# Norm factor and index relu applied in PSUM, forgetting rows as products over 32 partitions, T5 rows copied in two halves

## The chip, the cores and the metric

One core of a Trainium2 chip. The metric is the device time of one execution in microseconds; the kernel before was timed three times, and a further execution of it was profiled.

## The reference

One layer of a decoder trunk over 512 tokens of width 1024, everything in float32:

```
xn = rmsnorm(x, norm_mix_g)
sb, moba, fox, dsa and index parts = split(xn @ w_in)
o_sb   stick-breaking attention        4 heads of 64
o_mb   block-sparse attention, T5 bias 4 heads
o_fx   softmax(q k / 8 + c[t] - c[s]) v, c = cumsum(log_sigmoid(f))   4 heads
o_ds   I[t,s] = sum_h w[t,h] relu(q_idx[t,h] . k_idx[s]);  top 128 keys of I per query,
       softmax with T5 bias over them  4 heads, shared k and v
x  = x + (sum_i sigmoid(xn @ w_gate[i]) * (o_i @ w_branch[i])) @ w_out
x  = x + conv_ffn(rmsnorm(x, norm_ffn_g));   out = rmsnorm(x, norm_final_g)
```

## The kernel before

Activations lie with channels on the partitions and the 512 tokens along the free dimension. Products keep float32 accuracy by halves: an operand is split into a rounded high part (a cast on ScalarE) and the rest (a difference on VectorE or GpSimd), and three products are summed. A dense tile is 8 x 3 matmuls of 128x128 against 512 columns (`dense_steps`, L116). Weights are loaded by SyncE into two raw buffers `wr` and split into three pairs `wh`, `wl` (L91 to L104).

The stages: load and norm of x with the first value projection; then index and key projections; then the attention, in which 16 heads (F0, S0, F1, S1, M0, M1, D0, D1, two heads each) are worked off in steps n = 0, 1, 2, ..., with dense tiles of the projections and gates put between their parts; then the branch, output and feed-forward products. TensorE's order is that of the program text (`manual_schedule`); on the other engines and on SyncE's queue a planner sets the order by priorities and readiness.

In a step, `slot(n, pos, us)` (L662) runs what is due of earlier heads (transposes one step later, products with the values two steps later), then `dense(us)` of projections in the order of `ORDER`; between the slots stand the four score tiles of the step's head and, while there are any, index scores: `IXN` (L882) says how many behind each of the first positions, and the last entry holds for all later ones. When the 24 index scores are given out, the steps of the top-k search (L430) start. `QUOTA` gives the dense time of each slot.

PSUM has two banks "mm" for the dense tiles, used in turn, and six "a" for everything else.

- `factored` (L263) multiplies a projection's bank by the norm factor `rstd` into an SBUF tile `t...` of the ring "ir" (three buffers). `qtile`, `ktile` and `ixtile` (L311 to L340) cast that tile into halves on ScalarE and take the differences on VectorE (L317, L319, L329, L339); for k a transfer per head then fills the other 64 partitions (L330).
- `index_score` (L413): one matmul into a bank `ip`, a relu on ScalarE into an "ir" tile, then on VectorE a product with the head's weight added to `isc` (L423, L425).
- Forgetting rows: the cumulated logarithms `ch` and their negatives `cn` stand on partitions 96 to 99. `fox_rows` (L389) transfers them to rows 0 to 3 of each of four groups of 32 partitions, in `ck` and `cr`; for each head, VectorE multiplies `cr` by a column that is one in the head's group and zero elsewhere (L395). L458 adds the product `cq[h]` x `ck` over 128 partitions to the scores.
- `ix_spread` (L403) reads the index rows back from DRAM (`iqd`) by eight transfers. The T5 rows `brd` are copied to 128 rows for each of eight heads in `bdram` (L625), from where `bias_head` (L397) reads a head's matrix; the first is read at step 6.

Of the kernel before, what the change touches and what calls it, by code (L numbers as in the profile page):

```python
# [16 lines left out]
P = 128  # L17
# [32 lines left out]
def trunk(ctx: ExitStack, tc: tile.TileContext, xt, wv0, wv, wp, wdk, wg, wb, wo, wu, wd,  # L50
# [14 lines left out]
    ident = cst[:, 0:P]  # L65
    onesd = cst[:, 3 * P:4 * P]
    gn = cst[:, 4 * P:4 * P + 3 * KT]
    rowm = cst[:, 4 * P + 3 * KT:NCST]
    trir = cp.tile([P, P], F32R, name="trir")
    idr = cp.tile([P, P], F32R, name="idr")  # L70
    mskr = cp.tile([P, P], F32R, name="mskr")
# [3 lines left out]
    dpool = ctx.enter_context(tc.tile_pool(name="dpool", bufs=1, space=bass.MemoryType.DRAM))  # L75
    iqd = dpool.tile([8, 32, 2, S], F32, name="iqd")
    brd = dpool.tile([8, 640], F32, name="brd")
    bdram = dpool.tile([8, P, 640], F32, name="bdram")
    V.memset(eps, EPS)
    V.memset(one1, 1.0)  # L80
    V.memset(fr(negr), -1.0)
# [97 lines left out]
    with ExitStack() as ph:  # L179
# [80 lines left out]
            yield from dense_steps(ps[:m], hi, lo, blocks_of(xhi), blocks_of(xlo))  # L260
            return ps[:m]

        def factored(ps, name):  # L263
            m = ps.shape[0]
            t = pp.tile([P, S], F32, name=f"t{name}", tag="ir", bufs=3)
            V.tensor_tensor(out=t[:m], in0=ps, in1=rstd[:m], op=OP.mult)
            return t

        def drain(gen):
            while True:  # L270
                try:
                    next(gen)
                except StopIteration as e:
                    return e.value
# [4 lines left out]
        T.matmul(ms, onesd, sqa, start=True, stop=True)  # L279
        dkp = drain(dk)  # L280
        rms_rstd(ms, S, "m", pp, rstd, tag="ot")
        dkp = factored(dkp, "dk")
        for tt in range(NB):
            jk = pp.tile([P, P], F32, name=f"jk{tt}", tag="ot")
            V.tensor_tensor_reduce(out=jk, in0=rstd[:, tt * P:(tt + 1) * P], in1=ident, scale=1.0, scalar=0.0,
# [23 lines left out]
        qk, kdma = {}, [None]  # L309

        def qtile(name, scale):  # L311
            ps = factored((yield from proj(name)), name)
            q = pp.tile([P, 2, S], F32R, name=f"q{name}", tag="q", bufs=2)
            qk[name] = q
            A.activation(q[0:64, 0], ps[0:64], AF.Copy, scale=scale)
            A.activation(q[64:128, 1], ps[64:128], AF.Copy, scale=scale)
            V.scalar_tensor_tensor(out=q[64:128, 0], in0=ps[0:64], scalar=scale, in1=fr(q[0:64, 0]),  # L317
                                   op0=OP.mult, op1=OP.subtract)
            V.scalar_tensor_tensor(out=q[0:64, 1], in0=ps[64:128], scalar=scale, in1=fr(q[64:128, 1]),  # L319
                                   op0=OP.mult, op1=OP.subtract)  # L320

        def ktile(name):
            ps = factored((yield from proj(name)), name)
            k = pp.tile([P, 2, 2, S], F32R, name=f"k{name}", tag="k", bufs=2)
            qk[name] = k
            for h in range(2):
                r, o = slice(64 * h, 64 * h + 64), slice(64 - 64 * h, 128 - 64 * h)
                A.copy(k[r, h, 0], ps[r])
                V.tensor_tensor(out=k[r, h, 1], in0=ps[r], in1=fr(k[r, h, 0]), op=OP.subtract)  # L329
                kdma[0] = SP.dma_start(fr(k[o, h]), fr(k[r, h]))  # L330
# [2 lines left out]
        iq = {}  # L333

        def ixtile(c):
            t = factored(drain(proj(f"ix{c}")), f"ix{c}")
            hl = pp.tile([P, 2, S], F32R, name=f"iqs{c}", tag="lo", bufs=HB)
            A.copy(hl[:, 0], t)
            V.tensor_tensor(out=hl[:, 1], in0=t, in1=fr(hl[:, 0]), op=OP.subtract)  # L339
            SP.dma_start(iqd[4 * c:4 * c + 4].rearrange("h b x s -> (h b) x s"), fr(hl))  # L340
# [37 lines left out]
        A.copy(ch[R4, 0], fw[R4, 0])  # L378
        V.tensor_tensor(out=ch[R4, 1], in0=fw[R4, 0], in1=fr(ch[R4, 0]), op=OP.subtract)
        A.activation(cn[R4], fr(ch[R4]), AF.Copy, scale=-1.0)  # L380
        cr = pp.tile([P, S], F32, name="cr", tag="mix", bufs=KT)
        ck = pp.tile([P, S], F32R, name="ck", tag="mix", bufs=KT)
        cq = [pp.tile([P, S], F32R, name=f"cq{h}", tag="mix", bufs=KT) for h in range(4)]
        G.memset(cr, 1.0)
        G.memset(fr(ck), 1.0)

        ixtile(1)

        def fox_rows():  # L389

            for r in range(2):
                SP.dma_start(cr[2 + r:P:32], fr(cn[96:100, r]))
                SP.dma_start(fr(ck[r:P:32]), fr(ch[96:100, r]))
            for h in range(4):
                V.tensor_scalar(out=cq[h], in0=cr, scalar1=rowm[:, h:h + 1], scalar2=None, op0=OP.mult)  # L395

        def bias_head(h):  # L397
            e = pp.tile([P, S], F32, name=f"e{h}", tag="e", bufs=3)
            r = bdram[h].rearrange("p y -> (p y)")
            SP.dma_start(e, r[127:127 + P * 639].rearrange("(p y) -> p y", y=639)[:, :S])  # L400
            return e

# [10 lines left out]
        def index_score(i, h):  # L413
            n = P * (i + 1)
            if h == 0:
                isc[i] = pp.tile([P, n], F32, name=f"isc{i}")
            t = isc[i]
            ps = bank(f"ip{i}{h}")[:, :n]
            T.matmul(ps, iq[h][:, i * P:(i + 1) * P], ixk[:, :n], start=True, stop=True)
            r = pp.tile([P, S], F32, name=f"ir{i}{h}", tag="ir", bufs=3)[:, :n]  # L420
            A.activation(r, ps, AF.Relu)
            if h == 0:
                V.tensor_scalar(out=t, in0=r, scalar1=ixw[:, i, 0:1], scalar2=None, op0=OP.mult)  # L423
            else:
                V.scalar_tensor_tensor(out=t, in0=r, scalar=ixw[:, i, h:h + 1], in1=t, op0=OP.mult, op1=OP.add)  # L425
            if h == 7:
                G.affine_select(out=t[:, i * P:], in_=t[:, i * P:], pattern=[[-1, P]], base=0, channel_multiplier=1,
                                compare_op=OP.is_ge, fill=INADM)
# [15 lines left out]
        def softmax_head(b, h, q, k, v, bias, fox=False):  # L444
            p, hh = divmod(h, 2)
            nm = "FMSD"[b] + str(h)

            def scores():
                z = pp.tile([P, ALLQ], F32, name=f"z{nm}", tag="z", bufs=2)
                st = pp.tile([P, 3, NB], F32, name=f"st{nm}", tag="st", bufs=2)  # L450
                for i in range(NB):
                    n = P * (i + 1)
                    qs = slice(i * P, (i + 1) * P)
                    ps = bank(f"s{nm}{i}")[:, :n]
                    T.matmul(ps, q()[:, hh, qs], k()[:, 0, :n], start=True, stop=False)
                    T.matmul(ps, q()[:, hh, qs], k()[:, 1, :n], start=False, stop=not fox)
                    if fox:
                        T.matmul(ps, cq[h][:, qs], ck[:, :n], start=False, stop=True)  # L458
                    zz = z[:, QOFF[i]:QOFF[i] + n]
                    anchor[0] = V.tensor_tensor_reduce(out=zz, in0=ps, in1=bias(hh, i, n), scale=1.0, scalar=3e38,  # L460
                                           op0=OP.add, op1=OP.min, accum_out=st[:, 0, i:i + 1])
                    last_exp[0] = A.activation(zz, zz, AF.Exp, scale=-1.0, bias=st[:, 0, i:i + 1],
                                               accum_out=st[:, 1, i:i + 1])
                    V.reciprocal(st[:, 2, i:i + 1], st[:, 1, i:i + 1])
                    G.tensor_tensor(out=zz, in0=zz, in1=st[:, 2, i:i + 1].to_broadcast([P, n]), op=OP.mult)
                    yield
                box["z"] = z

            def turn():
                z = box["z"]  # L470
                ph_ = pp.tile([P, ALLQ], F32R, name=f"ph{nm}", tag="hi", bufs=HB)
                pl_ = pp.tile([P, ALLQ], F32R, name=f"pl{nm}", tag="lo", bufs=HB)
                for j in range(NB):
                    n = S - P * j
                    pt = bank(f"pt{nm}{j}")[:, :n]
                    for i in range(j, NB):
                        T.transpose(pt[:, (i - j) * P:(i - j + 1) * P],  # L477
                                    z[:, QOFF[i] + P * j:QOFF[i] + P * (j + 1)], ident)
                    sl = slice(KOFF[j], KOFF[j] + n)
                    A.copy(ph_[:, sl], pt)  # L480
                    anchor[0] = V.tensor_tensor(out=pl_[:, sl], in0=pt, in1=fr(ph_[:, sl]), op=OP.subtract)
                box["w"] = ph_, pl_

            box = {}
            return scores, turn, lambda: pv(b, p, hh, v(), *box["w"], nm)
# [134 lines left out]

        step = [-1]
        fox_rows()
        ix_spread()
        require("F0k")
        SP.dma_start(bdram, brd.rearrange("p (o y) -> p o y", o=1).to_broadcast([8, P, 640]))  # L625
        oTf = pp.tile([P, 2, S], F32, name="oTf")
        oTr = pp.tile([P, 3, 2, S], F32, name="oTr", tag="oT3")
        oT = [oTf, oTr[:, 0], oTr[:, 1], oTr[:, 2]]
# [46 lines left out]
        n = 0  # L675
        while due or n < len(heads):
            step[0] = n
            for h in EBIAS.get(n, ()):
                with tc.issue_after(kdma[0].ins):
                    ebias[h] = bias_head(h)  # L680
# [199 lines left out]
QUOTA = [1.5, 0.5, 2, 0.5, 1, 1]  # L880

LAG = [((1, 1), (2, 1)), ((1, 3), (2, 3))]  # L882
IXN = [0, 2, 3, 3, 2]
TKS = [1.2] * 16
EBIAS = {6: (0, 1), 8: (2,), 10: (3,), 11: (4, 5), 12: (6,), 14: (7,)}
NCST = 4 * P + 3 * KT + 4

# ---- launch
# [93 lines left out]
```

## Time and profile before

| | us |
|---|---|
| median of three timed runs | 879.92 (879.18 to 881.20) |
| the profiled execution | 877.93 |
| its span | 875.9 |
| TensorE busy | 844.6 |
| VectorE busy | 559.9 |
| ScalarE busy | 398.1 |
| GpSimd busy | 164.3 |

[...] PE is TensorE's matmul part, PEld its weight loads, DVE VectorE, ACT ScalarE, POOL GpSimd, SPq SyncE's queue.

### The profile page before, as it was taken

What the parts mean: (1) busy time and instruction counts of PE and PEld (TensorE: products, weight loads), DVE (VectorE), ACT (ScalarE), POOL (GpSimd) and SP (SyncE); (2) the same over time, 40 slices, a digit from 0 to 9 for tenths busy, and PEclk for the clock granted to TensorE, in tenths of its full rate; (3) what the DMA queues carried; (4) which work ended last, traced back from release to release, by engine and by line L of the source; (5) the groups of instructions that cost most, each with busy time, mean ns of one, the idle gap of its engine ahead of it and who ended that gap; (6) DMA issues with size and microseconds to landing.
All of it is one profiled execution on the core that took longest, in us unless ns stands there. A gap on an engine that the chain in (4) does not pass through costs nothing.

```text
span 875.9 us, 10670 instructions
## 1 busy us (share of the span) xinstructions
PE 844.6 (96%) x4040; PEld 710.4 (81%) x4040; DVE 559.9 (64%) x933; ACT 398.1 (45%) x608; POOL 164.3 (19%) x119
## 2 busy tenths in 40 slices
PE   8968999999998999999999999999999999999995
PEld 7757888788887888888888888888888888888885
DVE  6845899999663458645554477777777777423334
ACT  6524776666454573223334454444444444323221
POOL 0023547357558610000001200000000000000001
PEclk9987999999999999999999999999999999999998
DMA  6577130423523234224223233233333323333222
GB/s 222 154 241 186 53 95 26 121 61 105 172 85 110 71 97 127 90 89 129 72 73 97 97 94 99 97 97 97 96 97 97 97 96 91 91 91 108 85 67 97
DMA packets 31651, 91.18 MB, mean 104 GB/s; under 512 B 3376, under 2 KB 8368, under 8 KB 31600
## 3 DMA queue, kind: packets, MB, share of 16 engines
q1 hardware_dynamic: 30512, 89.45, 33.7%
q10 hardware_dynamic: 1088, 1.05, 0.4%
q8 instruction: 32, 0.52, 0.2%
q14 instruction: 19, 0.16, 0.1%
HBM read 83.75 MB, written 5.79 MB: 102 GB/s over the span
## 4 chain that ended last, share of the span: by engine, by line
PE 76%; DVE 12%; DMA 3%; ACT 3%; issue 2%; POOL 2%; SPq 0%; DVEq 0%; ACTq 0%
PE u L122 27%; PE dg L122 18%; PE dn L823 14%; PE o L122 5%; PE b L122 5%; DVE isc L437 2%; DVE m L436 2%; PE vpsVS L303 1%; DMA cr<-cn 1%; DMA kF0k<-kF0k 1%; DVE a L522 1%; DMA xr<-in_xt 1%; POOL ep L564 1%; PE dD0q L122 1%; PE ptD L477 0%
## 5 line engine op out<-in xcount | busy, mean ns | idle before, releaser
L92 ACT CAST wh<-wr 128x1024 fp32r<-128x1024 f32 (+1 forms) x129 | 133.5, 1038 | 159.8 <-PE dn L823 70.4
L93 DVE TENSOR_TENSOR wl<-wr,wh 128x1024 fp32r<-128x1024 f32 (+2 forms) x97 | 116.4, 1201 | 140.1 <-ACT wh L92 64.5
L93 POOL TENSOR_TENSOR wl<-wr,wh 128x1024 fp32r<-128x1024 f32 x32 | 77.7, 2431 | 70.8 <-ACT wh L92 26.1
L122 PE MATMUL u<-xhi,wh 128*128 128x512 f32 x352 | 87.5, 390 | 0.0
L122 PE MATMUL u<-xlo,wh 128*128 128x512 f32 x352 | 87.1, 389 | 0.0
L122 PE MATMUL u<-xhi,wl 128*128 128x512 f32 x352 | 87.1, 389 | 0.0
L799 DVE SCALAR_TENSOR_TENSOR cv<-h,cvp,cv 128x511 f32<-128x511 f32 x88 | 66.0, 751 | 26.1 <-ACT cv L797 24.6
L122 PEld LDWEIGHTS u<-xhi,wh 128*128 128x128 f32 x352 | 66.1, 188 | 14.1 <-issue 0.5
L122 PEld LDWEIGHTS u<-xlo,wh 128*128 128x128 f32 x352 | 66.1, 188 | 13.7
L122 PEld LDWEIGHTS u<-xhi,wl 128*128 128x128 f32 x352 | 66.1, 188 | 13.7
L823 PE MATMUL dn<-mh,wh 128*128 128x512 f32 (+1 forms) x198 | 72.9, 368 | 0.0
L823 PE MATMUL dn<-ml,wh 128*128 128x512 f32 (+1 forms) x198 | 72.3, 365 | 0.0
L823 PE MATMUL dn<-mh,wl 128*128 128x512 f32 (+1 forms) x198 | 72.3, 365 | 0.0
L797 ACT ACTIVATE cv<-h,cvp 128x512 f32<-128x512 f32 x44 | 35.9, 815 | 79.9 <-DVE h L795 79.9
L835 POOL TENSOR_TENSOR x<-x,yl 128x512 f32<-128x512 f32 x2 | 3.5, 1754 | 359.8 <-issue 354.4
L122 PE MATMUL dg<-xlo,wh 128*128 128x512 f32 x256 | 66.1, 392 | 0.0
L122 PE MATMUL dg<-xhi,wh 128*128 128x512 f32 x256 | 64.9, 390 | 0.0
L122 PE MATMUL dg<-xhi,wl 128*128 128x512 f32 x256 | 64.3, 390 | 0.0
L122 PEld LDWEIGHTS dg<-xhi,wl 128*128 128x128 f32 x256 | 47.7, 188 | 9.7
L122 PEld LDWEIGHTS dg<-xhi,wh 128*128 128x128 f32 x256 | 47.8, 188 | 9.4
L122 PEld LDWEIGHTS dg<-xlo,wh 128*128 128x128 f32 x256 | 47.4, 188 | 9.5
L771 POOL TENSOR_TENSOR rstd<-rstd,sqo 128x512 f32<-128x512 f32 x7 | 9.1, 1299 | 186.8 <-ACT sqo L770 186.8
(426 smaller groups left out, 1529.2 us busy)
## 6 DMA issues: line engine op xcount, KB each, us to landing
wr<-in_wu SPq DMA_DIRECT2D x44, 512.0 KB
wr<-in_wg SPq DMA_DIRECT2D x32, 512.0 KB
wr<-in_wp SPq DMA_DIRECT2D x16, 512.0 KB
wr<-in_wd SPq DMA_DIRECT2D x16, 512.0 KB
wbr<-in_wb SPq DMA_DIRECT2D x8, 512.0 KB
wr<-in_wo SPq DMA_DIRECT2D x8, 512.0 KB
wr<-in_wd SPq DMA_DIRECT2D x8, 384.0 KB
bdram<-brd SPq DMA_DIRECT2D x1, 2560.0 KB
```

Source lines behind the costliest of these rows:

```text
L92: A.copy(hi, raw)
L93: eng.tensor_tensor(out=lo, in0=raw, in1=fr(hi), op=OP.subtract)
L122: T.matmul(o, a[:, k], b(k), start=(n == 0), stop=(n == len(todo) - 1))
L303: T.matmul(ps, a[:, k, ts_], b, start=(m == 0), stop=(m == 3 * KT - 1))
L436: V.max(out=m8, in_=t)
L437: V.match_replace(out=t, in_to_replace=m8, in_values=t, imm_value=MARK)
L522: anchor[0] = V.scalar_tensor_tensor(out=a[:, o0:o0 + n], in0=zt, scalar=0.0, in1=a[:, o0:o0 + n], op0=OP.max, op1=OP.add)
L564: G.tensor_tensor(out=t, in0=e, in1=isc[i], op=OP.add)
L771: G.tensor_tensor(out=acc, in0=acc, in1=sq, op=OP.add)
L797: A.activation(c, h, AF.Identity, scale=cvp[:, i, 2:3], bias=cvp[:, i, 3:4])
L799: V.scalar_tensor_tensor(out=c[:, x:], in0=h[:, :S - x], scalar=cvp[:, i, 2 - x:3 - x], in1=c[:, x:], op0=OP.mult, op1=OP.add)
L823: T.matmul(o, a, b[:, k, cs], start=(n == 0 and m == 0), stop=(n == ND - 1 and m == 2))
```

## The change

`factored` multiplies in place, in the PSUM bank, and the casts and differences read the bank. The index relu is also done in place, and VectorE reads the bank. The "ir" tiles of both go.

`cr` and the four `cq` go. `cq` and `ck` are cleared by GpSimd, with rows 0 to 3 of each group of 32 partitions set to one; the transfers write the rows into them, and the product of a head runs over its 32 partitions.

`ix_spread` now stands behind the projection F0k, its transfers tied to follow the last transfer of F0k. The copy to `bdram` is made in two halves of four heads at the beginning of steps 2 and 5, each tied behind the last key transfer given out so far. `IXN` puts the first index scores two positions later (0, 0, 2, 3, then 3 each, in place of 0, 2, 3, 3, then 2 each).

```diff
-    bdram = dpool.tile([8, P, 640], F32, name="bdram")
+    bdram = [dpool.tile([4, P, 640], F32, name=f"bdram{i}") for i in range(2)]
...
-        def factored(ps, name):
-            m = ps.shape[0]
-            t = pp.tile([P, S], F32, name=f"t{name}", tag="ir", bufs=3)
-            V.tensor_tensor(out=t[:m], in0=ps, in1=rstd[:m], op=OP.mult)
-            return t
+        def factored(ps):
+            V.tensor_tensor(out=ps, in0=ps, in1=rstd[:ps.shape[0]], op=OP.mult)
+            return ps
...
-        cr = pp.tile([P, S], F32, name="cr", tag="mix", bufs=KT)
+        cq = pp.tile([P, S], F32R, name="cq", tag="mix", bufs=KT)
         ck = pp.tile([P, S], F32R, name="ck", tag="mix", bufs=KT)
-        cq = [pp.tile([P, S], F32R, name=f"cq{h}", tag="mix", bufs=KT) for h in range(4)]
-        G.memset(cr, 1.0)
-        G.memset(fr(ck), 1.0)
+        for t in (cq, ck):
+            G.memset(fr(t), 0.0)
+            for h in range(4):
+                G.memset(fr(t[32 * h:32 * h + 4]), 1.0)
...
-                SP.dma_start(cr[2 + r:P:32], fr(cn[96:100, r]))
+                SP.dma_start(fr(cq[2 + r:P:32]), fr(cn[96:100, r]))
                 SP.dma_start(fr(ck[r:P:32]), fr(ch[96:100, r]))
-            for h in range(4):
-                V.tensor_scalar(out=cq[h], in0=cr, scalar1=rowm[:, h:h + 1], scalar2=None, op0=OP.mult)
...
-            r = pp.tile([P, S], F32, name=f"ir{i}{h}", tag="ir", bufs=3)[:, :n]
-            A.activation(r, ps, AF.Relu)
+            A.activation(ps, ps, AF.Relu)
             if h == 0:
-                V.tensor_scalar(out=t, in0=r, scalar1=ixw[:, i, 0:1], scalar2=None, op0=OP.mult)
+                V.tensor_scalar(out=t, in0=ps, scalar1=ixw[:, i, 0:1], scalar2=None, op0=OP.mult)
             else:
-                V.scalar_tensor_tensor(out=t, in0=r, scalar=ixw[:, i, h:h + 1], in1=t, op0=OP.mult, op1=OP.add)
+                V.scalar_tensor_tensor(out=t, in0=ps, scalar=ixw[:, i, h:h + 1], in1=t, op0=OP.mult, op1=OP.add)
...
-                        T.matmul(ps, cq[h][:, qs], ck[:, :n], start=False, stop=True)
+                        T.matmul(ps, cq[32 * h:32 * h + 32, qs], ck[32 * h:32 * h + 32, :n], start=False, stop=True)
...
         fox_rows()
-        ix_spread()
         require("F0k")
-        SP.dma_start(bdram, brd.rearrange("p (o y) -> p o y", o=1).to_broadcast([8, P, 640]))
+        with tc.issue_after(kdma[0].ins):
+            ix_spread()
...
             step[0] = n
+            if n in BCOPY:
+                i = BCOPY.index(n)
+                with tc.issue_after(kdma[0].ins):
+                    SP.dma_start(bdram[i], brd[4 * i:4 * i + 4].rearrange("p (o y) -> p o y", o=1).to_broadcast([4, P, 640]))
...
-IXN = [0, 2, 3, 3, 2]
+IXN = [0, 0, 2, 3, 3]
+BCOPY = (2, 5)
```

## Rows read from the trace of the kernel before

**Rows 1.** The page's first part: engine, busy us, share of the span, instructions.

```profile
PE 844.6 (96%) x4040; PEld 710.4 (81%) x4040; DVE 559.9 (64%) x933; ACT 398.1 (45%) x608; POOL 164.3 (19%) x119
```

**Rows 2.** Waits of TensorE, 58 to 340 us: us in total, times, longest.

```profile
PE dS0k L122 <- DVE tF0k L266: 6.8, 1, 6.8
PE sF L455 <- DMA kF0k<-kF0k: 3.3, 1, 3.3
PE ptF L477 <- POOL zF L465: 3.2, 4, 1.0
PE ptD L477 <- POOL zD L465: 2.5, 1, 2.5
PE zb L512 <- DVE oTf L496: 2.3, 2, 1.4
```

**Rows 3.** Timeline of TensorE, 47 to 84 us: start, us, operation, [idle before <-releaser].

```profile
47.51 1.98 PE L122 MATMUL dF0k<-xhi,wh 128*128 128x512 f32 x8
...
52.95 1.98 PE L122 MATMUL dS0q<-xhi,wh 128*128 128x512 f32 x8
...
65.37 3.75 PE L122 MATMUL dS0k<-xhi,wh 128*128 128x512 f32 x8 [6.82 <-DVE tF0k L266]
...
83.74 0.34 PE L455 MATMUL sF<-kF0k,qF0q 128*128 128x384 f32 x1
```

**Rows 4.** Stretches: length; busy (instructions) by engine PE, PEld, DVE, ACT, POOL; clock, DMA.

```profile
66.00:68.00 2.00, 2.00 (x6) 1.58 (x5) 1.94 (x3) 1.56 (x2) 0.34 (x1) 0.50 1.08 213
100.00:220.00 120.00, 114.04 (x644) 99.38 (x644) 115.78 (x269) 79.99 (x141) 70.58 (x41) 1.00 0.30 86
```

**Rows 5.** The chain that ended last, 18 to 100 us: start, us, what.

```profile
49.80 10.94 DMA cr<-cn
...
60.87 3.75 DVE cq L395 x4
...
66.62 8.92 DMA kF0k<-kF0k
```

**Rows 6.** Timeline of SyncE's queue: transfers issued, start and us of the issue.

```profile
41.69 0.77 SPq L625 DMA_DIRECT2D bdram<-brd x1
42.56 4.79 SPq L340 DMA_DIRECT2D iqd<-iqs x1
...
61.71 3.70 SPq L407 DMA_DIRECT2D iq<-iqd x8
```

**Rows 7.** VectorE by shape, 18 to 340 us: busy us, mean ns, idle before.

```profile
L425 DVE SCALAR_TENSOR_TENSOR isc<-ir,ixw,isc 128x384 f32<-128x384 f32 x7 | 7.9, 1129 | 0.4 <-ACT ir L421 0.2
...
L481 DVE TENSOR_TENSOR plF<-ptF,phF 128x512 fp32r<-128x512 f32 x4 | 2.7, 675 | 0.0
...
L329 DVE TENSOR_TENSOR kF0k<-tF0k,kF0k 64x512 fp32r<-64x512 f32 x2 | 1.4, 687 | 0.7 <-ACT kF0k L328 0.7
```

**Rows 8.** Last readers of a tile and next users of its bank: tile view, timelines.

```profile
47.17 0.69 DVE L339 TENSOR_TENSOR iqs<-tix,iqs 128x512 fp32r<-128x512 f32 x1 [1.77 <-ACT iqs L338]
...
L329 DVE TENSOR_TENSOR kM0k<-tM0k,kM0k x2: 690/1734/2779, 178.2 to 181.5; 64x512 fp32r<-64x512 f32 x2
...
179.22 1.17 PE L303 MATMUL vpsVM<-wh,xhi 128*128 128x256 f32 x8
```

**Rows 9.** A stretch of the differences for k (L329) alone, VectorE, as rows 4.

```profile
83.00:220.00 137.00, 13.31 (x10) 1.00 0.29 83
```

**Rows 10.** Timeline of TensorE's 32-row products, their weight loads and what follows.

```profile
35.32 1.24 PE L356 MATMUL bp<-vt,t5s 32*8 32x512 f32 x4
36.49 2.11 PE L122 MATMUL dix<-xhi,wh 128*128 128x512 f32 x8
...
35.76 0.09 PEld L356 LDWEIGHTS bp<-vt,t5s 32*8 32x8 f32 x1 [0.34 <-DVE ixw L290]
```

**Rows 11.** Timeline: two index scores on TensorE, and index sums on VectorE.

```profile
99.23 0.51 PE L419 MATMUL ip<-ixk,iq 128*128 128x384 f32 x2
...
105.00 2.31 DVE L425 SCALAR_TENSOR_TENSOR isc<-ir,ixw,isc 128x384 f32<-128x384 f32 x2
```

More of the change, by code (lines that the diff above doesn't have):

```diff
@@ L67, in trunk @@
     gn = cst[:, 4 * P:4 * P + 3 * KT]
-    rowm = cst[:, 4 * P + 3 * KT:NCST]
     trir = cp.tile([P, P], F32R, name="trir")
@@ L281, in trunk @@
         rms_rstd(ms, S, "m", pp, rstd, tag="ot")
-        dkp = factored(dkp, "dk")
+        dkp = factored(dkp)
         for tt in range(NB):
@@ L311, in qtile @@
         def qtile(name, scale):
-            ps = factored((yield from proj(name)), name)
+            ps = factored((yield from proj(name)))
             q = pp.tile([P, 2, S], F32R, name=f"q{name}", tag="q", bufs=2)
@@ L322, in ktile @@
         def ktile(name):
-            ps = factored((yield from proj(name)), name)
+            ps = factored((yield from proj(name)))
             k = pp.tile([P, 2, 2, S], F32R, name=f"k{name}", tag="k", bufs=2)
@@ L335, in ixtile @@
         def ixtile(c):
-            t = factored(drain(proj(f"ix{c}")), f"ix{c}")
+            t = factored(drain(proj(f"ix{c}")))
             hl = pp.tile([P, 2, S], F32R, name=f"iqs{c}", tag="lo", bufs=HB)
@@ L391, in fox_rows @@
             for r in range(2):
-                SP.dma_start(cr[2 + r:P:32], fr(cn[96:100, r]))
+                SP.dma_start(fr(cq[2 + r:P:32]), fr(cn[96:100, r]))
                 SP.dma_start(fr(ck[r:P:32]), fr(ch[96:100, r]))
-            for h in range(4):
-                V.tensor_scalar(out=cq[h], in0=cr, scalar1=rowm[:, h:h + 1], scalar2=None, op0=OP.mult)
         def bias_head(h):
             e = pp.tile([P, S], F32, name=f"e{h}", tag="e", bufs=3)
-            r = bdram[h].rearrange("p y -> (p y)")
+            r = bdram[h // 4][h % 4].rearrange("p y -> (p y)")
             SP.dma_start(e, r[127:127 + P * 639].rearrange("(p y) -> p y", y=639)[:, :S])
```

## The prediction

> **What bounds the kernel now.** I read the page first: TensorE is busy 844.6 of 875.9 us [rows 1]. So a change away from TensorE can pay only where TensorE stands still or runs at its lower clock, and the next view is the list of what TensorE waits for between 58 and 340 us [rows 2]: one wait of 6.8 us for VectorE's tF0k, one of 3.3 us for the transfer into kF0k, and seven short ones of 8.0 us together (behind VectorE's oTf, GpSimd's zF and zD). After 340 us the timeline shows no such gap before the last tile.
>
> The two long waits are neighbours, so I followed them in TensorE's timeline [rows 3]. dS0q ends at 65.37 - 6.82 = 58.55; the third score tile of head F0 starts at 83.74. Between these lie 25.2 us. The work in them at full speed: a dense tile of 24 matmuls takes 52.95 - 47.51 = 5.44 us, that is 0.443 ns a column, and besides S0k's tile there are 384 + 768 columns of scores, 1,024 of index scores and 6,144 of values, 3.7 us. So 9.1 us of work took 25.2: **16.1 us are lost here**. [...]
>
> The chain of waits names the cause [rows 5]: 10.94 us for the 8-KB rows cr<-cn, then four products cq on VectorE (3.75 us), with tF0k and kF0k queued behind them on the same engine, then 8.92 us for kF0k's transfer. SyncE's queue tells why small transfers take so long [rows 6]: the 2,560-KB copy of bdram is issued at 41.69, the next issue (iqd) takes 4.79 us, and the eight iq transfers (2 MB) are issued at 61.71, just ahead of kF0k; the DMA share is 1.08 at 213 GB/s [rows 4].
>
> From 100 to 220 us VectorE is the fullest engine (115.78 of 120) and TensorE loses 6.0 us [rows 4].
>
> **The change part by part.**
>
> *Forgetting rows.* The transfers now write cq and ck directly; the four products go, and with them the wait of VectorE for a transfer. tF0k's product then runs when dF0k ends (52.95). Its two casts and two differences, 0.69 us each at most [rows 7], overlap to about 2.1 us: kF0k is complete at about 56.2. ix_spread is now tied behind kF0k's last transfer, and bdram has left the stretch, so kF0k is not behind 4.5 MB. TensorE asks for it after dS0q and 18 matmuls of S0k, at 58.55 + 4.1 = 62.7. Even at the old 8.92 us it would land at 65.1, 2.4 late; with an empty queue in time. I take 0. The eight more memsets on GpSimd lie in its idle time ahead of its first weight half: 0; without that cover they would delay that half, and with it S0q's tile.
>
> *New waits of the front.* A projection tile's bank is now free only after its last reader, not after the product. F0k's bank was index tile ix1's, whose last difference ends at 47.17 + 0.69 = 47.86 [rows 8] against a start of 47.51 [rows 3]: +0.4. The index rows: the first index score moves two positions back, to 62.7 + 0.2 + 1.4 + 0.3 + 2.7 + 0.5 = 67.8 by columns. 2 MB at 213 GB/s take 9.6 us from about 57: 66.8, or 69.3 with one 512-KB weight load between. I take +1.0 (0 to 3.9, two loads). **Front: -16.1 + 0.4 + 1.0 = -14.7.**
>
> *Factor and relu in PSUM.* VectorE's differences for q and k and its index sums now read one operand from PSUM. Where both lie in SBUF, they are stretched while GpSimd works: L329 takes 13.31 us for ten [rows 9] against 0.687 each undisturbed, and the 384-wide index sum takes 1.129 although a 512-wide difference with a PSUM operand takes 0.675 [rows 7]. At these prices VectorE is relieved of 13.3 - 6.9 = 6.4 and of 7 x 0.45 = 3.2 us, 9.6 at least. But on TensorE no more than its 6.0 us of gaps can come back. The 2.3 behind oTf are VectorE's; the 3.2 behind zF are GpSimd's, which waits for VectorE and also has weight halves to do. I take **-2.5** (0 to -6). D's 2.5 us come from GpSimd: unchanged.
>
> [...]
>
> No row shows VectorE or ScalarE writing to PSUM. The nearest are the same operations into SBUF, and I take those, 0 more; at 0.1 us each, 40 such writes would cost 4 on engines with that much relief.
>
> *Banks.* Each later q and k tile holds its bank until the last difference. Against the start of the next user of that bank I found room everywhere but at M0k: its last difference ends at 182.2, the second value tile of M starts at 179.22 [rows 8], 3.0 late; without the stretch of 2.1 about 0.9. Index scores hold a bank until VectorE has added them. Together +1.5 (0 to 9).
>
> *32-row products.* 16 matmuls shrink from 128 rows to 32 at the same column count. The only 32-row rows are bp's: four matmuls with 1,280 columns, 0.57 us, take 36.49 - 35.32 = 1.17; 0.34 of the rest is a wait for VectorE [rows 10], 0.26 remain. [...] I take 0.15 each, between nothing and the row: **+2.4** (0 to 9.6 at 0.60, if the row's wait belongs to it too).
>
> *bdram in two halves* at steps 2 and 5, SyncE. Each is 1,280 KB, 6 us at 213 GB/s; queued behind it are weight loads and kF1k or kS1k. The DMA share is 0.30 from 100 to 220 [rows 4] and weights are fetched two tiles ahead; first use is at step 6. +0.4 (0 to 4).
>
> **Sum:** -14.7 - 2.5 + 1.5 + 2.4 + 0.4 = -12.9, call it -13. The profiled execution took 877.93 (2.0 around its span): 864.9. The median of the three timed runs, 879.92, is 2.0 above it, so **866.9** for the timed runs.
>
> **The rivals.**
> - *More of the middle comes back*: all 6.0 of the gaps, nothing for banks and 32 rows: 16.1 - 1.4 + 6.0 - 0.4 = 20.3 gained, 859.6. For it: VectorE's relief is larger than the gaps. Against: GpSimd's part.
> - *Index rows late*: three weight loads ahead of the iq transfers and kF0k's second transfer, 3.9 us of wait, after which the clock falls again (0.50 after a wait of this size [rows 2, 4]) and some 5 us are lost to it: 7.9 more than taken, 874.8. It is also the case of a planner that leaves the queue as full as it was, so that the change does only half of what it says.
> - *32 rows at the full price*: 0.60 x 16 = 9.6, 7.2 more: 874.1. [...]
> - *Slower: index banks.* The scores issued at 99.23 were added only by 107.3 [rows 11], 7.6 us after their matmul. A bank held so long, with six banks and three scores a position, makes TensorE wait some 3.8 us a position (step 1 uses 20 banks in some 12.5 us of columns, so six go round in 3.8) at the seven positions of steps 1 and 2: +27, 893. It decides where VectorE's lag exceeds one round of the banks. Against: the lag arises under stretched sums, which the change relieves.
>
> **How the numbers follow.** Forecast 0.52, more comes back 0.18, index rows late 0.12, 32 rows 0.08, index banks 0.06, the rest (a cancelled gain by several small waits, within 0.2%) 0.04. The range has to reach the first three rivals: 859 to 875.5; left out are the banks, the rest and some tails. 0.2% (1.8 us) is about what a measurement tells from no change. Faster 0.90, same 0.04, slower 0.06.
>
> **What would show it.** Right: no TensorE wait over 1 us between 58 and 68 us, clock 1.00 throughout, the first F score near 63 us, the row of the wait for tF0k gone; L329 near 0.69 each. Wrong: waits for iq, a DMA share near 1 past 68 us, TensorE waits behind isc in steps 1 and 2, gaps around L458. If the front gains 15 but the end does not, the middle gave it back, and rows of VectorE between 85 and 205 us would show where.

## The result and the profile after

| | before | after |
|---|---|---|
| median of four timed runs, us | 879.55 (877.19 to 881.20) | 864.34 (863.31 to 866.64) |
| the profiled execution, us | 877.93 | 866.64 |
| its span, us | 875.9 | 864.9 |
| TensorE busy, us | 844.6 | 848.5 |
| VectorE busy, us | 559.9 | 539.2 |

The ratio is 0.9833, with an interval from 0.9801 to 0.9865: faster, 15.2 us by the medians. The profiled execution of after is the slowest of its four; the other three took 863.31, 863.42 and 865.26. A fall of the clock that, by the times, not every execution has may be part of that difference (below). Between the two profiled executions there are only 877.93 - 866.64 = 11.3 us, and the readings of the traces explain these, not the 15.2. The first part of the page, against [rows 1]:

```profile
PE 848.5 (98%) x4040; PEld 709.6 (82%) x4040; DVE 539.2 (62%) x929; ACT 396.7 (46%) x608; POOL 165.2 (19%) x127
```

TensorE does the same 4,040 matmuls in 3.9 us more busy time and yet ends 11 us earlier, so it stands still less. What it waits for between 18 and 340 us (us in total, times, longest), against [rows 2]:

```profile
PE ip L415 <- DMA iq<-iqd: 1.5, 1, 1.5
PE vpsVM L300 <- DVE vvM L210: 1.4, 1, 1.4
PE dF0k L121 <- DVE iqs L336: 0.5, 1, 0.5
PE ip L415 <- DVE stF L455: 0.2, 1, 0.2
PE ptF L472 <- POOL zF L460: 0.2, 1, 0.2
```

Both long waits are gone, and so are nearly all the short ones: behind oTf, zF, zM (0.5 in before) and also zD. New ones stand in their place, for the index rows, for a bank ahead of the second value tile of M, for F0k's bank, and a small one behind stF. The front in TensorE's timeline (start, us, operation, idle before), against [rows 3]:

```profile
47.74 2.11 PE L121 MATMUL dF0k<-xhi,wh 128*128 128x512 f32 x8 [0.49 <-DVE iqs L336]
...
53.31 1.98 PE L121 MATMUL dS0q<-xhi,wh 128*128 128x512 f32 x8
...
58.75 1.98 PE L121 MATMUL dS0k<-xhi,wh 128*128 128x512 f32 x8
...
62.83 0.22 PE L450 MATMUL sF<-kF0k,qF0q 128*128 128x128 f32 x1
...
70.80 0.70 PE L415 MATMUL ip<-ixk,iq 128*128 128x512 f32 x2 [1.46 <-DMA iq<-iqd]
```

dS0k follows dS0q without a gap, and the first score tile starts at 62.83, in before at 75.68. The clock granted to TensorE, as a share of its full speed, does not stay at 1.00, though. Stretches (length; busy and instructions by engine; clock, DMA share, GB/s), against [rows 4]:

```profile
58.00:68.00 10.00, 10.00 (x56) 8.46 (x55) 4.59 (x12) 4.53 (x10) 5.64 (x4) 1.00 1.04 221
...
72.00:74.00 2.00, 2.00 (x7) 0.96 (x5) 1.49 (x3) 0.98 (x3) 0.32 (x1) 0.55 1.07 313
74.00:76.00 2.00, 2.00 (x7) 1.66 (x7) 1.20 (x3) 1.12 (x3) 0.51 (x1) 0.50 1.02 295
100.00:220.00 120.00, 118.46 (x654) 101.62 (x653) 103.76 (x270) 77.29 (x135) 69.44 (x41) 1.00 0.35 107
```

Behind the stop of 1.46 us it falls to 0.50 for some 7 us. From 100 to 220 us VectorE's busy time fell from 115.78 to 103.76, and TensorE stands still for 1.5 us instead of 6.0. SyncE's queue (start and us of the issue), against [rows 6]:

```profile
46.38 1.07 SPq L390 DMA_DIRECT2D cq<-cn  x2
...
55.57 0.53 SPq L327 DMA_DIRECT2D kF0k<-kF0k  x1
...
57.48 5.44 SPq L403 DMA_DIRECT2D iq<-iqd  x8
...
71.25 0.69 SPq L676 DMA_DIRECT2D bdram<-brd  x1
```

The first transfer of kF0k is issued at 55.57, the second at 56.91, and the index rows follow it. Last, VectorE by shape (busy us, mean ns, idle before), against [rows 7]:

```profile
L420 DVE SCALAR_TENSOR_TENSOR isc<-ip,ixw,isc 128x384 f32<-128x384 f32 x7 | 4.3, 614 | 0.1
...
L326 DVE TENSOR_TENSOR kF1k<-dF1k,kF1k 64x512 fp32r<-64x512 f32 x2 | 1.4, 680 | 0.0
```

The 384-wide index sum takes 614 ns instead of 1,129, and a difference for k 680 where it was stretched to as much as 2,779 [rows 8]. Of M0k's two differences in before the stretched one runs beside an operation of GpSimd, the other while GpSimd is idle. In after, with one operand in PSUM, a difference beside the same operation takes 0.67 us:

```profile
177.50 2.96 POOL L527 TENSOR_TENSOR ll<-a,lh 128x1280 fp32r<-128x1280 f32 x1
...
178.23 2.78 DVE L329 TENSOR_TENSOR kM0k<-tM0k,kM0k 64x512 fp32r<-64x512 f32 x1
...
181.51 0.69 DVE L329 TENSOR_TENSOR kM0k<-tM0k,kM0k 64x512 fp32r<-64x512 f32 x1
```

```profile
112.04 2.97 POOL L522 TENSOR_TENSOR ll<-a,lh 128x1280 fp32r<-128x1280 f32 x1
...
112.79 0.67 DVE L326 TENSOR_TENSOR kF1k<-dF1k,kF1k 64x512 fp32r<-64x512 f32 x1
```

### The profile page after: what moved, and what is told of

It reads as the page before. It is cut to its first block, busy times and chain, and to the rows that moved or that the text cites. A ratio compares the mean times of both kernels' runs of the same rounds, so it can differ in the third digit from the quotient of the medians.

```text
span 864.9 us, 10652 instructions
## 1 busy us (share of the span) xinstructions
PE 848.5 (98%) x4040; PEld 709.6 (82%) x4040; DVE 539.2 (62%) x929; ACT 396.7 (46%) x608; POOL 165.2 (19%) x127
## 4 chain that ended last, share of the span: by engine, by line
PE 81%; DVE 0%; ACT 0%; DVEq 0%; issue 0%
PE u L121 28%; PE dg L121 19%; PE dn L822 14%; PE o L121 5%; PE b L121 5%; PE vpsVM L300 1%; PE dM1q L121 1%; PE dM0k L121 1%; PE zb L533 1%; PE dD1q L121 1%; PE dM1k L121 1%; PE dD0q L121 1%; PE ptM L472 1%; PE ptD L472 1%; PE dM0q L121 0%; PE oD L488 0%
```

## The experiments

In all of them the time is the median in us, with the lowest and highest run; "before" was run on the same chip in the same series.

**The changed kernel once more** (e7_changed_again), in the series of the kernels that take one part alone.

> The changed kernel itself, to stand beside the parts on the same chip. Expected 862 to 865. If the fall of the clock behind the 1.5 us wait is not the same in every execution, its times spread by some 3 us, while the kernel with the index scores one position later spread by less than 0.5.

Measured: 863.64 (863.49 to 866.80), before 879.18; ratio 0.9827 (0.9808 to 0.9845). The five executions took 863.49, 863.56, 863.64, 865.36 and 866.80. The slowest, which is the profiled one, has a mean granted clock of 0.991, the one of 865.36 has 0.994 and the three fastest 0.995 to 0.996. So the fall behind the wait for the index rows seems to come in some executions and not in others, and to cost 2 to 3 us where it comes. That the fast ones lack it is concluded from their times and mean clocks, since none of them was profiled.

**Only the PSUM part, on the kernel before** (e4_psum_only):

```diff
-            t = pp.tile([P, S], F32, name=f"t{name}", tag="ir", bufs=3)
-            V.tensor_tensor(out=t[:m], in0=ps, in1=rstd[:m], op=OP.mult)
-            return t
+            V.tensor_tensor(out=ps, in0=ps, in1=rstd[:ps.shape[0]], op=OP.mult)
+            return ps
...
-            A.activation(r, ps, AF.Relu)
+            A.activation(ps, ps, AF.Relu)
```

> The kernel before with one part of the change alone: norm factor and index relu in PSUM. Theory (the relief of VectorE is worth the gaps of the attention, some 6 to 9 us, and the front stays late): 877.8 - 7 = 871, with the 6.8 us wait near S0k still there and TensorE waits after 85 us under 3 us. Rival (VectorE's relief is worth something only where the front is early): 877.8, the waits behind oTf and zF still there. Second rival (S0k's bank, now held to F0k's last difference, and the index banks cost more than the relief gives): 879 and more.

Measured: 869.64 (869.06 to 872.75), before 879.18; ratio 0.9895 (0.9878 to 0.9913), or 9.5 us. TensorE's three longest waits, 18 to 340 us:

```profile
PE dS0k L122 <- DVE kF0k L327: 7.0, 1, 7.0
PE sF L452 <- DMA kF0k<-kF0k: 3.7, 1, 3.7
PE vpsVM L301 <- DVE vvM L211: 1.3, 1, 1.3
```

The two long waits are untouched, so this gain is in the main not the front's. What the trace shows of it lies in the attention: 8.5 us of short waits there became 2.8. The wait for zD is gone with no edit near GpSimd. That is not the whole of the 9.5: the profiled execution is the slowest of its six, only 5.2 below the profiled one of before, and from 13 to 17 us its clock is 0.57 on the mean, where before has 1.00. Where the other 4 us of the timed runs lie, no trace shows.

The wait at vpsVM comes with this part, and with it alone (before, e3 and e5 don't have it). How it arises is read in after, on TensorE and VectorE:

```profile
172.54 1.21 PE L300 MATMUL vpsVM<-wh,xhi 128*128 128x256 f32 x8 [1.36 <-DVE vvM L210]
```

```profile
172.99 0.69 DVE L326 TENSOR_TENSOR kM0k<-dM0k,kM0k 64x512 fp32r<-64x512 f32 x1
```

M0k's bank is still read at 172.99, when the second value tile is under way. So that tile has the other bank, and waited for it until the first value tile's last reader, vvM, ended at 172.48. In before M0k's bank came free with the factor, at 177.2, ahead of the second tile's start at 179.22.

**The changed kernel without the PSUM part** (e3_sbuf), the same edit the other way round on the changed kernel: factor and relu write SBUF tiles again.

> The changed kernel with the norm factor and the index relu written to SBUF again, as before; all else as changed. Theory (reading one operand from PSUM frees VectorE of 9.6 us and more of stretched instructions, and this is what gave back the 6.5 us of gaps in the attention): 864.3 + 6 = 870, with TensorE waits of 5 us and more between 85 and 325 us and differences for k again near 1.3 us each. Rival (the gaps went because the stages lie otherwise to each other, VectorE's relief does not matter): 864.3, waits under 3 us although the differences are stretched. The front stays as changed in both.

Measured: 873.81 (873.43 to 874.27), before 877.82; ratio 0.9950 (0.9935 to 0.9964). That is some 9.5 us slower than the changed kernel (by the ratios, 0.0117 x 879 = 10.3). TensorE's waits from 58 to 325 us, and the stretched difference among VectorE's operations by shape:

```profile
PE vpsVS L302 <- DVE vvS L210: 3.1, 1, 3.1
PE ptD L475 <- POOL zD L463: 2.5, 1, 2.5
PE zb L510 <- DVE oTf L494: 1.4, 2, 0.9
PE oF L490 <- ACT ir L419: 0.7, 1, 0.7
```

```profile
L328 DVE TENSOR_TENSOR kM1k<-t,kM1k 64x512 fp32r<-64x512 f32 x2 | 3.7, 1861 | 0.7 <-ACT kM1k L327 0.7
```

The difference for k is back at 1,861 ns, the waits for zD and oTf are back, and new ones stand for the ring "ir". The clock is 0.50 from 81 to 84 us, behind the wait for vvS, and 0.72 on the mean from 264 to 270, behind the stop of 2.5, so in this execution these stops cost more than themselves. In the profiled execution of before the same stop of 2.5 left the clock at 1.00. Both directions agree on the size in the timed runs: the PSUM part is worth 9 to 10 us, and more than the theory's 6. What no run separates is the factor from the relu, and the operand's place from the ring "ir" of three buffers, which goes and comes back with it.

**Only the halves of bdram, on the kernel before** (e5_bdram_only): the copy at L625 goes, and the two copies at steps 2 and 5 come, as in the diff of the change.

> The kernel before with one part alone: the bdram copy in two halves at steps 2 and 5. Theory (the copy is what makes the small row transfers take 10.9 us, and VectorE only stands behind them): the rows land about 8 us earlier, the 6.8 us wait near S0k goes, what stays is kF0k behind the index rows with some 3 us and the clock: 877.8 - 9 = 869. Rival (the products cq on VectorE hold the chain whatever the transfers do): under 3 us gained, 875 and more.

Measured: 870.81 (868.45 to 872.89), before 879.18; ratio 0.9906 (0.9887 to 0.9925), or 8.4 us, close to the theory's 9. SyncE's queue and TensorE's two longest waits:

```profile
46.58 1.07 SPq L392 DMA_DIRECT2D cr<-cn  x2
...
51.44 3.95 SPq L407 DMA_DIRECT2D iq<-iqd  x8
...
58.17 2.43 SPq L330 DMA_DIRECT2D kF0k<-kF0k  x2
```

```profile
PE sF L455 <- DMA kF0k<-kF0k: 4.6, 1, 4.6
PE ptF L477 <- POOL zF L465: 3.4, 4, 1.7
```

The wait of 6.8 us for tF0k is gone although the four products on VectorE are still there: the 8-KB rows arrive in time once the 2,560-KB copy is not ahead of them. What is left in the front is the wait for kF0k, issued behind the index rows; the attention's waits are as before.

**Only the forgetting rows, on the kernel before** (e6_rows_only): the rows are written directly, without VectorE's products, but over 128 partitions, so that no 32-row product is in it. Each head has its own `cq`, and each transfer of a row of `cn` becomes four.

```diff
-                SP.dma_start(cr[2 + r:P:32], fr(cn[96:100, r]))
+                for h in range(4):
+                    SP.dma_start(fr(cq[h][32 * h + 2 + r:32 * h + 3 + r]), fr(cn[96 + h:97 + h, r]))
...
-            for h in range(4):
-                V.tensor_scalar(out=cq[h], in0=cr, scalar1=rowm[:, h:h + 1], scalar2=None, op0=OP.mult)
```

> The kernel before with one part alone: the forgetting rows are transferred straight into four tiles cq over 128 partitions (eight one-row transfers in place of two, no product on VectorE, no 32-row matmul); bdram and index rows stay where they were. Theory (what holds the front is VectorE waiting in order for the rows): the 6.8 us wait goes, kF0k is ready near 56 us and its transfer is late only by what bdram leaves in the queue, so 8 to 12 us gained: 866 to 870. Rival (the queue is the cause, kF0k's transfer still lands near 75 us behind bdram and the index rows): under 3 us gained, 875 and more.

Measured: 883.68 (880.85 to 885.11), before 879.18; ratio 1.0049 (1.0030 to 1.0067): slower by 4.5 us, as the rival had it, for which the queue is the cause. SyncE's queue, then TensorE's longest wait:

```profile
57.73 4.26 SPq L394 DMA_DIRECT2D cq<-cn  x6
...
62.66 5.05 SPq L407 DMA_DIRECT2D iq<-iqd  x8
69.49 2.21 SPq L330 DMA_DIRECT2D kF0k<-kF0k  x2
```

```profile
PE sF L455 <- DMA kF0k<-kF0k: 15.7, 1, 15.7
```

VectorE no longer waits for the rows, but six of the transfers are issued only at 57.73, the index rows behind them, and kF0k behind both at 69.49. TensorE then stands still for 15.7 us in one piece, and from 68 to 85 us its clock is 0.54 on the mean. With the large copy in front, taking the products away only moves the wait. The four-fold number of transfers may have its share in that: this run does not tell what the rows of the change, with two transfers, would do alone.

**Rows over 128 partitions in the changed kernel** (e1_rows128), the same edit on the changed kernel; **index scores later** (e2_ix_later); **both** (e9_both):

```diff
-IXN = [0, 0, 2, 3, 3]
+IXN = [0, 0, 0, 3, 3]
```

> The changed kernel, but each head's forgetting product runs again over 128 partitions: four tiles cq, cleared, with ones in their own group, are written directly by eight one-row transfers in place of two; no product on VectorE. Theory (a 32-row matmul between 128-row ones costs TensorE some 0.38 us more, 16 of them 6.1 us): 864.3 - 6.1 = 858.2, and the stretch from the first S1q matmul to the first M0q matmul shrinks from 29.8 to about 26.7 us. Rival (the longer stretch has another cause, the 32 rows cost nothing): 864.3, and the stretch stays near 29.8. Second rival (only the 0.15 us of the prediction): 861.9.

> The changed kernel with the index scores one more position back (none in the first three positions of step 0, three behind the fourth, then three each as now). Theory (the 1.5 us wait for the index rows is what lets the clock fall, and the seven us at half clock behind it cost 3.5 more): 864.3 - 5.0 = 859.3, and the granted clock is 1.00 from 72 to 80 us. Rival (the clock falls for another reason, for instance the gaps around the 32-row products): only the wait goes, 862.8, and the clock still falls. Second rival (the scores then pile up in step 1 and VectorE's lag makes TensorE wait): no gain, 864 to 867.

> The changed kernel with both edits: forgetting products over 128 partitions written directly, and the index scores one position later. Theory (the two costs are separate): 864.3 - 6.1 - 5.0 = 853.2. Rival (they overlap: without the gaps of the 32-row products the clock would not have fallen, or the front is bound by the index rows all the same): 856 to 859.

Measured, before 877.82: e1 860.87 (860.21 to 861.15), ratio 0.9801 (0.9783 to 0.9819); e2 862.34 (862.26 to 862.64), ratio 0.9819 (0.9801 to 0.9837); e9 859.37 (859.10 to 859.77), ratio 0.9785 (0.9767 to 0.9803).

The 32-row products cost 862.34 - 859.37 = 3.0 us in the timed runs, and 864.34 - 860.87 = 3.5 between the change and e1, across two chips. Their price on TensorE is read in the stretch from S1q's first matmul to M0q's, with 145 matmuls, eight of them forgetting products, in after and then in e9 (columns as in [rows 4]):

```profile
120.55:150.34 29.79, 29.79 (x145) 23.39 (x144) 27.40 (x67) 18.23 (x34) 19.23 (x11) 1.00 0.37 126
115.11:142.32 27.21, 26.96 (x145) 23.24 (x144) 26.33 (x67) 17.66 (x33) 18.57 (x10) 1.00 0.42 142
```

By the lengths that is 0.32 each, or 5.2 for sixteen; without the 0.25 us that TensorE stands still in e9's stretch it is 0.35. TensorE's busy time over the whole program, 844.8 in e2 and 840.0 in e9, gives 0.30. Of the 2.2 between 5.2 and 3.0, waits that are longer in e9 than in e2 explain 1.3 (0.9 for zF instead of 0.2, and 1.1 ahead of index scores instead of 0.5); 0.9 stay unassigned.

The times miss the theories' sums: e1 lies between its theory (858.2) and its second rival (861.9), e2 lies 3.0 above its theory (859.3), and e9 far above its theory (853.2) and 0.4 above its rival (856 to 859). They had taken the whole fall of the clock off a median in which, by the times, only some executions have it, and the products' whole price on TensorE. Between the profiled executions of after and e2 there are 866.64 - 862.49 = 4.2 us, near the 5.0 that e2's theory took off. One product in the two timelines, after and then e9:

```profile
125.51 0.28 PE L451 MATMUL sF<-kF1k,qF1q 128*128 128x256 f32 x1
125.72 0.38 PE L453 MATMUL sF<-ck,cq 32*128 32x256 f32 x1
126.03 1.65 PE L121 MATMUL dS1q<-xhi,wl 128*128 128x512 f32 x6
```

```profile
119.73 0.28 PE L452 MATMUL sF<-kF1k,qF1q 128*128 128x256 f32 x1
119.85 0.28 PE L454 MATMUL sF<-ck,cq 128*128 128x256 f32 x1
119.97 1.55 PE L121 MATMUL dS1q<-xhi,wl 128*128 128x512 f32 x6
```

From the start of the matmul ahead to the start of the one behind there are 0.52 us with 32 rows and 0.24 with 128.

As e2's theory had it, its profiled execution has no wait for the index rows, and no fall of the clock from 58 to 80 us. Its two-microsecond stretch, against the same one of after above:

```profile
74.00:76.00 2.00, 2.00 (x19) 2.00 (x19) 1.56 (x4) 0.88 (x3) 1.04 (x1) 1.00 1.03 209
```

Its five runs lie within 0.4 us, those of after within 3.3. e9 is the best version found, and faster than both kernels. In it the forgetting products run over 128 partitions.

**A second 32-row product behind each** (e10_two32), on e2. The added product is of a cleared tile and adds zeros.

```diff
-                        T.matmul(ps, cq[32 * h:32 * h + 32, qs], ck[32 * h:32 * h + 32, :n], start=False, stop=True)
+                        T.matmul(ps, cq[32 * h:32 * h + 32, qs], ck[32 * h:32 * h + 32, :n], start=False, stop=False)
+                        T.matmul(ps, zr[32 * h:32 * h + 32, qs], ck[32 * h:32 * h + 32, :n], start=False, stop=True)
```

> The changed kernel with the index scores one position later (862.3), and behind each 32-row forgetting product a second 32-row product of the same width, of a cleared tile, which adds zeros. Theory (what costs is the change between 128-row and 32-row products, once per group): the second product costs only its columns, on average 320 x 0.443 ns = 0.14 us, 16 of them 2.3 us: 864.6; in TensorE's timeline the two 32-row products follow each other at the distance of their columns. Rival (each 32-row matmul costs 0.33 us more by itself): 862.3 + 2.3 + 5.2 = 869.8, and the distance is the columns plus 0.2 and more.

Measured: 864.14 (863.97 to 864.35), before 879.80; ratio 0.9827 (0.9806 to 0.9849). Against e2, which ran on another chip, that is 1.8 us by the medians and 0.7 by the ratios (0.0008 x 879) for sixteen products of 5,120 columns together, whose columns alone take 5,120 x 0.443 ns = 2.3. The same place in its timeline:

```profile
122.39 0.28 PE L453 MATMUL sF<-kF1k,qF1q 128*128 128x256 f32 x1
122.60 0.38 PE L455 MATMUL sF<-ck,cq 32*128 32x256 f32 x1
122.82 0.28 PE L456 MATMUL sF<-ck,zr 32*128 32x256 f32 x1
123.03 1.67 PE L121 MATMUL dS1q<-xhi,wl 128*128 128x512 f32 x6
```

The stretch from S1q's first matmul to M0q's, in e2 and then in e10, holds eight of the added products:

```profile
116.29:146.07 29.78, 29.78 (x144) 23.38 (x143) 27.66 (x68) 18.32 (x34) 19.22 (x11) 1.00 0.39 131
117.38:148.22 30.84, 30.84 (x153) 24.28 (x152) 28.74 (x69) 18.45 (x34) 19.12 (x11) 1.00 0.38 126
```

It grew by 1.06 us, and the columns of eight, 2,560, take 1.13 (one of e2's matmuls is missing from its count). So a product over 32 rows is not dear in itself: the second one adds no more than its columns. From start to start the two lie 0.22 apart, 0.11 more than their columns, but the way back to 128 rows is then 0.21 instead of 0.31. What costs is a lone product, going from 128 rows to 32 and back: 0.52 us from start to start in after, 0.24 over 128 rows in e9. Why the change of rows takes this time, no run shows.

**PSUM part and halves of bdram together, on the kernel before** (e11_psum_bdram = e4 + e5), with the old forgetting rows and the index rows still ahead of kF0k.

> The kernel before with two parts of the change: norm factor and relu in PSUM, and bdram in two halves at steps 2 and 5. The forgetting rows are as before, with their four products on VectorE and 128 rows on TensorE, and the index rows and scores are placed as before. Theory (the two parts stand for separate losses, the attention's gaps and the transfers of the front, 9.5 and 8.4 us): 879 - 17.9 = 861, so the whole change's 863.6 is reached without its 32-row products. Rival (the early front needs VectorE free of the cq products as well): 866 and more.

Measured: 864.84 (863.58 to 865.68), before 879.80; ratio 0.9834 (0.9811 to 0.9857), between what the two theories gave. The parts do not quite add up: 9.5 + 8.4 = 17.9 alone, 15.0 together. But these two alone reach the time of the whole change. TensorE's longest wait:

```profile
PE sF L452 <- DMA kF0k<-kF0k: 3.1, 1, 3.1
```

**The same with the direct rows over 128 partitions** (e12_old_ix_order = e11 + the edit of e6). It differs from e9 in the order of the index rows and in `IXN`.

> The same with the forgetting rows transferred straight into four tiles over 128 partitions (no products on VectorE); so it differs from the fastest kernel so far (859.4) only in that the index rows are fetched ahead of F0k's transfer and the index scores begin one position after the start of step 0, as before. Theory (2 MB of index rows ahead of kF0k's transfer make TensorE wait some 4 us for it, and the clock falls behind that wait): 859.4 + 4 to 8 = 863 to 867. Rival (with VectorE free, kF0k is issued early enough to go ahead of the index rows): 859.4.

Measured: 865.13 (864.45 to 866.68), before 879.80; ratio 0.9843 (0.9819 to 0.9866), as the theory had it. It is no faster than e11 (864.84): with the large copy moved, taking the products off VectorE, with eight row transfers instead of two, gains nothing by itself. TensorE's longest wait, and SyncE's queue:

```profile
PE sF L452 <- ACT wh L92: 5.6, 1, 5.6
```

```profile
52.44 4.88 SPq L405 DMA_DIRECT2D iq<-iqd  x8
...
59.91 0.53 SPq L328 DMA_DIRECT2D kF0k<-kF0k  x1
```

The wait is named after ScalarE, whose weight cast ended last, at 68.78. But kF0k's first transfer, which the first score needs, is issued only at 59.91, in after at 55.57, and kF0k's two transfers took 7.5 and 8.7 us to land, in after 3.0. So it landed at 68.6 at the latest, against the score's start at 68.79, and the trace does not tell safely which of the two was waited for; the weights of that cast, issued at 58.16, stand behind the index rows as well. Putting the index rows behind kF0k, with the scores later as in e9, is worth 865.13 - 859.37 = 5.8 us, across two chips (by the ratios 0.0058 x 879 = 5.1). With the change's own `IXN`, in e1, it is 865.13 - 860.87 = 4.3 (by the ratios 3.7).

In a row, by the medians and across chips: before 879.55; with the PSUM part and the halves of bdram 864.84 (e11); with direct rows over 128 partitions 865.13 (e12); with the index rows behind kF0k 860.87 (e1); with the products over 32 rows 864.34 (the change). Two parts made the gain, the order of the index rows added some 4 us, and the 32-row products gave most of that back.

## Why the prediction was right, point by point

The time, 864.34 against 866.9, lies in the range, and so does that of the profiled execution, 866.64 against 864.9. The front, which was named first, carried most of the 11.3 us between the profiled executions; in the timed runs the PSUM part is worth as much (9.5 alone, the halves of bdram 8.4). That the total came out close is in part luck: the front gave some 4 us less than its term and the 32-row products cost 1 to 3 more than theirs, while the PSUM part gave 7 more.

- **The front: the mechanism right, some 4 us too much in the profiled execution.** The first F score was forecast near 63 and came at 62.83; no wait over 1 us lies between 58 and 68 us; the row of the wait for tF0k is gone; F0k's bank costs 0.5 (0.4 forecast). The index rows came 1.5 late (1.0 forecast, of 0 to 3.9). What the sum left out is what follows such a stop: the clock, which the forecast had put only into the rival of the late index rows. At 0.50 for some 7 us it takes 3.5. The 16.1 lost before were 10.1 of waits and some 6 of clock, which is 0.50 in before from 62 to 71 and from 76 to 80 us. In their place stand 0.5 + 1.5 + 3.5: 10.6 won, where 14.7 were forecast. Four 32-row products, which the sum priced apart, take 1.3 of that, which leaves 9.3. The trace agrees: step 1's first score stands at 82.79, in before at 93.05, 10.3 earlier, with three index scores (0.7 us) deferred past it, which leaves 9.6. Without the fall the front would give 9.6 + 3.5 = 13.1. Two of the prediction's signs of being wrong came: this wait for iq, and a DMA share of 1.07 and 1.02 from 72 to 76 us. With the clock behind it the wait takes 5.0, so in this execution the rival of the late index rows (8.9) is true in part.
- **What frees the front was put too broadly.** The prediction counted the four products and the large copy as one cause. e5 and e6 separate them: moving the copy alone gives 8.4; taking the products away alone, with more transfers in their place, loses 4.5, and with the copy moved it changes nothing (e12 against e11). The order of the index rows, which the prediction counted only through "an empty queue", is worth some 4 with the change's index scores and 5 to 6 with those of e9.
- **Factor and relu in PSUM: the mechanism right, the term too small.** Taken was -2.5, with bounds of 0 and -6; e4 and e3 give 9.5 each way in the timed runs. Two steps failed. GpSimd's part was held against it, and D's 2.5 were called unchanged because the releaser is GpSimd; in fact nearly all of these waits went, those behind GpSimd too: ptF's and zb's went with ptD's. And the bound of 6.0 came from 100 to 220 us alone, while 8.5 us of such waits lie between 93 and 329 us; 1.8 are left in after. These waits are 6 to 7 of the 9.5. The rest is not placed; that a stop can cost clock besides its length is seen in e3, but not in the attention of before's profiled execution. The price of L326 was forecast at 0.69 and measured at 0.68 to 0.69.
- **PSUM as operand and as result: right.** A 64x512 difference reads PSUM in 680 to 690 ns (L326, means of two) and read SBUF undisturbed in 687. Nor does writing PSUM cost much, for which 0 was taken: the factor takes 700 ns (L263, mean of two) and took 686 into SBUF, and the relu of 512 columns 579 against 596 on ScalarE.
- **Banks: right.** 1.5 were taken; vpsVM waits 1.4 because M0k holds its bank, the one place that was named. No wait in steps 1 and 2 behind isc exceeds 0.2 us, so the slower rival (866.9 + 27 is 894, not 893) did not occur. The prediction held against it that the lag comes from stretched sums, and these are stretched no more.
- **32-row products: the term too small.** Taken was 0.15 each; measured were 0.30 to 0.35 on TensorE and 0.19 in the timed runs, still within the bounds of nothing and 0.60. The row of the four bp products [rows 10] had a price near this in it: they stand in succession, so the remainder of 0.26 can be read as that of one change to 32 rows and back, and each forgetting product makes both. Taken so, 0.26 each, the term would have been 4.2. The rival of 0.60 each was farther off; the 0.34 in it was a wait and no price.
- **bdram in halves: nothing seen.** The copies are issued at 71.25 and 116.11, and no wait stands behind them; 0.4 was taken.

After the front, from step 1's first score to the branch, after takes 234.9 us and before 236.0. In it are -6.7 of waits (8.5 to 1.8), +3.9 for twelve 32-row products and +0.7 for deferred index scores: -2.1 against -1.1 measured. The 1.0 between them is not assigned.

## What to carry to other kernels

Look for operations that take longer in one place than in another: here VectorE's index sums took 1,129 ns with both operands in SBUF and 614 with one in PSUM. Where several engines pass work around, relieving the fullest one can give back most of the short waits (8.5 us of them became 2.8 in e4), also those that the trace puts down to a neighbour: sum the waits over the whole stage before bounding the gain. A small transfer that many wait for should stand in the queue ahead of a large one that is needed late; moving the large one gave 8.4 us here, and taking away the work behind the small one nothing by itself (e12 against e11). A lone product over 32 rows between full ones saved nothing here and cost some 0.32 us of TensorE; fill the unused rows with zeros instead, as e9 does.

## What the runs showed of the hardware

- Behind a stop of 1.46 us the granted clock fell from 1.00 to 0.50 for some 7 us in the profiled execution of after. By the times, other executions of the same program did not have it (863.5 beside 866.8), and e1, which stops 1.9 us at the same place, keeps 1.00 from 72 to 80 us. A stop of 2.53 us for zD left 1.00 in before and was followed by 0.50 in e3. What decides it was not found.
- A lone 32-row product between 128-row ones costs some 0.32 us (0.30 to 0.35, after against e9 and e2 against e9), a second one behind it no more than its columns (1.06 us for eight, e10 against e2).
- Writing into the PSUM bank that is read next costs VectorE 14 ns for 512 columns (700 against 686) and ScalarE nothing (579 against 596), while it takes one operand off SBUF; the part of the change that does so is worth 9 to 10 us in this kernel.
